# Order of the rope's work beside attention in a two-layer trunk kernel

## The chip, the cores and the metric

The kernel runs on one core of a Trainium2 chip. The metric is the device time of one execution in microseconds (us), and the figure of a kernel is the median of its runs. The core has five engines that run side by side, each in the order of its own instruction stream, and wait for one another through semaphores: TensorE (PE, matrix products), VectorE (DVE, elementwise work and reductions), ScalarE (ACT, activations and copies), GpSimd (POOL, here mostly the issue of copies) and SyncE (SP, the issue of transfers).

## The reference

The reference is a trunk of two layers over 1024 positions of width 1024, in float32. Layer 0 is attention and an MLP, layer 1 a gated recurrence and an MLP, and a norm stands at the end. The change touches layer 0's attention alone:

```
qkv = h @ w_qkv                       # q, k: 8 heads x 2 components x 64
q = rope(q, positions) * (d ** -0.5)
k = rope(k, positions)
# rope: [t1 * cos - t2 * sin, t2 * cos + t1 * sin]
s = einsum('bqhcd,bkhcd->bhcqk', qb, k)      # two score maps a head
s = where(k_chunk <= q_chunk, s, -inf)
p = softmax(s)
a = p[:, :, 0] - lam * p[:, :, 1]
o = einsum('bhqk,bkhe->bqhe', a, v)
```

So each head needs its own projected q and k, turned by the rope, before its first score.

## The kernel before

**Three products for one.** A float32 product is made of three on PE with operands cut into a high and a low part (`split`, L336): high by high, high by low, low by high. For the scores the parts are laid on top of one another. A head's component has 64 rows, so high and low part fill the 128 rows of one operand: `stacked` (L695) builds such a tile with two copies by DMA from POOL's queue. A head needs two such tiles for q (`qs`, 4 copies) and four for k (`ks`, 8 copies, 256 KB each).

**Attention in 64 slots.** `attention` (L893) walks through 8 heads of 8 query blocks, one block a slot; the blocks of a head come in the order 4, 5, 6, 7, 0, 1, 2, 3 (`ORDER`). A slot s does: scores of its block on PE (`scores`, L749: two products into each of two accumulators, then a mask and a maximum on DVE, and the exponentials on ACT), the transposes of the block before it (L809 on PE, copied out by ACT in L987), the product with v of the block two before (L819), and `combine` (L789: three DVE instructions that join the two softmaxes). Between them PE is given `fills`: steps of the projections of later heads (L588 to L591), and towards the end of the output product. PE, ACT, DVE and POOL keep the order in which the program writes the instructions (`manual_schedule`, L958); SP's order comes from a scheduler.

**The rope's work.** When a projection of q or k of a later head is done, ACT copies it out (L713), four DMAs on SP's queue copy it with its halves swapped into a tile `sw` (L668), and then five steps follow: times cos in place (DVE, L679), `sw` times sin (DVE, L680), their sum (DVE, L676), the high part (ACT, L687), the low part (DVE, L690). The low part is followed by the stack's copies on POOL (L699, L700). The product with cos writes over q or k, which the swap's DMAs read; so it waits for them.

**The queue.** The DVE steps are not written where they become ready. `aside` (L865) puts each into a list, with the slot from which it may run: it counts forward from the present slot until the given time has passed, at 2.8 + 0.65 i us for a slot of block i. The time is `RS` (10) for cos, sin and sum, `RL` (2) for the low part. `run_aside` (L876) is called twice in a slot, once after the exponentials and once after `combine`, and each call runs one step (`ASIDE`): the first in the list that is due. New entries go to the end of the list. The list also holds the scaling of attention's outputs (`subln`, L824) and their low parts (L848).

Of the kernel before, what the change touches and what calls it, by code (L numbers as in the profile page):

```python
# [12 lines left out]
ALU = mybir.AluOpType  # L13
# [281 lines left out]
class Trunk:  # L295
# [375 lines left out]
    def rope(self, q, sw, then):  # L671

        nc = self.nc

        def add():
            nc.vector.tensor_tensor(out=q, in0=q, in1=sw, op=ALU.add)  # L676
            then()

        self.aside(RS, lambda: nc.vector.tensor_tensor(out=q, in0=q, in1=self.cos, op=ALU.mult))  # L679
        self.aside(RS, lambda: nc.vector.tensor_tensor(out=sw, in0=sw, in1=self.sin, op=ALU.mult))  # L680
        self.aside(RS, add)

    def parts_of(self, q, then):

        nc = self.nc
        h, l = self.t4("qkh", F32R), self.t4("qkl", F32R)
        nc.scalar.activation(out=h, in_=q, func=AF.Copy)  # L687

        def low():
            nc.vector.tensor_tensor(out=l, in0=q, in1=h.bitcast(F32), op=ALU.subtract)  # L690
            then(h, l)

        self.aside(RL, low)

    def stacked(self, name, first, second, c):  # L695

# [165 lines left out]
            s += 1  # L862
        self.tasks.setdefault(s, []).append(fn)

    def aside(self, us, fn):  # L865

        if self.slot is None:
            self.held.append(fn)
            return
        s = self.slot  # L870
        while us > 0:
            us -= 2.8 + 0.65 * ORDER[s % NT]
            s += 1
        self.queue.append((s, fn))

    def run_aside(self, n):  # L876
        for at, fn in list(self.queue):
# [609 lines left out]
        self.mlp(1, True)  # L1487


RS, RL, RN, RT, R3 = (10, 2, 3, 2, 3)  # L1490
ASIDE = (1, 1)
LAGS = (1, 2, 4)
FILL_PART = [(1.24, 1.17, 0.33), (0.74, 1.39, 0.4), (0.52, 1.0, 0.14), (0.74, 1.26, 0.4), (0.74, 1.0, 0.56), (0.79, 0.94, 0.37), (0.89, 1.18, 0.4), (1.04, 1.23, 0.4)]
# [37 lines left out]
```

## Time and profile before

| | |
|---|---|
| median of 3 runs | 2242.0 us (2241.39 to 2243.5) |
| the profiled execution | 2248.95 us, of which span 2247.2 us |
| PE busy | 2130.8 us (95%) |
| DVE busy | 1530.5 us (68%) |
| ACT busy | 1067.6 us (48%) |
| POOL busy | 100.1 us (4%) |
| mean granted TensorE clock | 0.981 |

Attention's first score stands at 116 us, its last at 567 us. A row of the timeline gives the start from the span's beginning, the duration, engine, line, operation, the tiles written and read, and in brackets the idle time of that engine just before, with what ended it. A row of waits gives what waited, for whom, the sum, how often and the longest. In the windows, busy time of each engine is followed by the number of its instructions; PEclk is the granted TensorE clock, where 1.00 is 2.4 GHz and 0.50 is 1.2 GHz.

### The profile page before, as it was taken

Reading aid. Unit: us, or ns where it says so; the run is one execution under the profiler, and the core shown is the slowest. Engines: PE = TensorE matmul, PEld = TensorE weight load, DVE = VectorE, ACT = ScalarE, POOL = GpSimd, SP = SyncE. Lnnn points to the kernel's source line nnn. Section 1 sums busy time; section 2 is a strip of 40 time slices with the busy share of each in tenths; the row PEclk is TensorE's granted clock in tenths of the full one; section 3 lists DMA queues with packets and bytes.
Section 4 is the critical chain, followed back from the end, with each engine's and each line's share of the span. In section 5 each row is a group of like instructions: output and inputs, shape, how many; then the busy total and the mean of one; then the engine's idle time right before and its main releaser. Section 6 shows DMA issues by size and latency. Waiting matters only on the chain.

```text
span 2247.2 us, 26498 instructions
## 1 busy us (share of the span) xinstructions
PE 2130.8 (95%) x9826; PEld 1758.0 (78%) x9826; DVE 1530.5 (68%) x2073; ACT 1067.6 (48%) x1627; POOL 100.1 (4%) x171
## 2 busy tenths in 40 slices
PE   8997999879999999899999999999899999899997
PEld 7786777768888888788887887777688888688885
DVE  5465676565896777577878477756967776486575
ACT  4344566456663444344435266635644443453343
POOL 3201111110000000000000000000000000000000
PEclk9998999999999999999999999999999999999998
DMA  6635353453634443597647322144244444874633
GB/s 188 175 88 130 97 143 101 123 152 109 211 116 142 155 155 134 190 353 280 218 158 240 90 78 84 36 159 132 94 151 155 150 150 169 322 263 166 217 128 135
DMA packets 239298, 355.82 MB, mean 158 GB/s; under 512 B 16225, under 2 KB 137154, under 8 KB 239170
## 3 DMA queue, kind: packets, MB, share of 16 engines
q1 hardware_dynamic: 230338, 326.87, 43.6%
q0 software_dynamic: 7680, 25.17, 4.8%
q10 hardware_dynamic: 1152, 2.10, 0.3%
q8 instruction: 77, 1.26, 0.2%
q14 instruction: 51, 0.42, 0.1%
HBM read 229.29 MB, written 91.23 MB: 143 GB/s over the span
## 4 chain that ended last, share of the span: by engine, by line
PE 60%; DVE 11%; ACT 7%; issue 3%; DMA 2%; POOL 0%; SPq 0%; ACTq 0%; POOLq 0%; DVEq 0%
PE acc L1219 5%; PE acc L1220 5%; PE acc L1221 5%; PE acc L144 4%; PE acc L145 4%; PE acc L143 4%; PE acg L1219 2%; PE acg L1221 2%; PE acg L1220 2%; PE acc L589 2%; PE acc L588 2%; PE acb L145 2%; PE acb L143 2%; PE acb L144 2%; PE acg L145 2%
## 5 line engine op out<-in xcount | busy, mean ns | idle before, releaser
L1121 ACT ACTIVATE ct<-ct 128x1024 f32<-128x1024 f32 x64 | 67.9, 1061 | 251.1 <-DVE ct L1190 250.1
L345 DVE TENSOR_TENSOR h2l<-h,h2h 128x1024 fp32r<-128x1024 f32 x112 | 136.6, 1220 | 65.6 <-ACT h2h L342 61.9
L766 ACT ACTIVATE p<-acc,nmax 128x768 f32<-128x768 f32 (+7 forms) x128 | 95.3, 744 | 143.1 <-DVE nmax L783 71.5
L588 PE MATMUL acg<-xgh,wh 128*128 128x512 f32 x384 | 161.6, 421 | 1.5 <-ACT vT L732 1.5
L589 PE MATMUL acg<-xgl,wh 128*128 128x512 f32 x384 | 152.7, 398 | 0.0
L591 PE MATMUL acg<-xgh,wl 128*128 128x512 f32 x384 | 152.7, 398 | 0.0
L342 ACT ACTIVATE h2h<-h 128x1024 fp32r<-128x1024 f32 x112 | 117.6, 1050 | 59.6 <-DMA h<-hid 51.3
L342 ACT ACTIVATE w2h<-w 128x1024 fp32r<-128x1024 f32 x80 | 84.3, 1054 | 88.0 <-DVE w L56 72.1
L143 PE MATMUL acc<-w2h,h2h 128*128 128x512 f32 x256 | 103.0, 402 | 13.9 <-ACT w2h L342 12.2
L143 PE MATMUL acc<-h2h,w2h 128*128 128x512 f32 x256 | 101.1, 395 | 7.5 <-ACT w2h L342 7.4
L418 POOL TENSOR_TENSOR rstd<-ms,mhalf 128x4 f32<-128x4 f32 (+2 forms) x25 | 22.4, 897 | 1900.0 <-DVE ms L416 1898.6
L144 PE MATMUL acc<-w2l,h2h 128*128 128x512 f32 x256 | 102.3, 400 | 2.8 <-DVE w2l L345 2.8
L1220 PE MATMUL acc<-t12l,w12h 128*128 128x512 f32 x256 | 100.7, 393 | 4.4 <-DVE t12l L345 4.4
L1190 DVE TENSOR_TENSOR cl<-cl,acc 128x512 f32<-128x512 f32 x64 | 60.8, 950 | 64.3 <-PE acc L1221 64.3
L345 DVE TENSOR_TENSOR w2l<-w,w2h 128x1024 fp32r<-128x1024 f32 x80 | 97.7, 1222 | 9.0 <-PE acc L144 4.9
L145 PE MATMUL acc<-h2h,w2l 128*128 128x512 f32 x256 | 100.9, 394 | 2.7 <-DVE w2l L345 2.7
L1219 PE MATMUL acc<-t12h,w12h 128*128 128x512 f32 x256 | 100.6, 393 | 3.1 <-DVE ct L1190 3.1
L145 PE MATMUL acc<-w2h,h2l 128*128 128x512 f32 x256 | 101.5, 396 | 0.0
L144 PE MATMUL acc<-h2l,w2h 128*128 128x512 f32 x256 | 100.8, 394 | 0.0
L1221 PE MATMUL acc<-t12h,w12l 128*128 128x512 f32 x256 | 100.2, 391 | 0.0
L762 PE MATMUL acc<-ks,qs 128*128 128x512 f32 (+2 forms) x192 | 67.8, 360 | 23.0 <-DMA ks<-qkh 23.0
L591 PEld LDWEIGHTS acg<-xgh,wl 128*128 128x128 f32 x384 | 73.8, 192 | 17.0 <-DVE wl L345 0.5
(383 smaller groups left out, 6004.4 us busy)
## 6 DMA issues: line engine op xcount, KB each, us to landing
w<-in_mlp_w_dram SPq DMA_DIRECT2D x96, 512.0 KB, 4.4
raw<-in_mlp_w_dram SPq DMA_DIRECT2D x64, 512.0 KB, 4.4
h<-hid SPq DMA_DIRECT2D x64, 512.0 KB, 5.2
h<-hid SPq DMA_DIRECT2D x96, 256.0 KB, 5.1
w<-in_mlp_w_dram SPq DMA_DIRECT2D x80, 256.0 KB, 3.9
hid<-cl SPq DMA_DIRECT2D x64, 256.0 KB, 2.3
hid<-h SPq DMA_DIRECT2D x32, 512.0 KB, 2.6
hid<-h SPq DMA_DIRECT2D x64, 256.0 KB, 2.4
```

Source lines behind the costliest of these rows:

```text
L143: mm(bank[m], ah, bh, start=first, stop=False)
L144: mm(bank[m], ah, bl, start=False, stop=False)
L145: mm(bank[m], al, bh, start=False, stop=end)
L342: nc.scalar.activation(out=hi, in_=src, func=AF.Copy)
L345: (lo_eng or nc.vector).tensor_tensor(out=lo, in0=src, in1=hi.bitcast(F32), op=ALU.subtract)
L588: mm(ps[:, pc], a, xh[:, cs], start=(k == 0), stop=False)
L589: mm(ps[:, pc], a, xl[:, cs], start=False, stop=False)
L591: mm(ps[:, pc], b, xh[:, cs], start=False, stop=(k == n - 1))
L766: nc.scalar.activation(out=p[c][:, :n], in_=src, func=AF.Exp, bias=nmax[:, c : c + 1], accum_out=sums[:, c : c + 1])
L1219: mm(bank, ah[:, k], bh, start=k == 0, stop=False)
L1220: mm(bank, ah[:, k], bl, start=False, stop=False)
L1221: mm(bank, al[:, k], bh, start=False, stop=k == 3)
```

## The change

Three edits in the queue: the product with cos gets the waiting time `RL` (2) instead of `RS`; `RS` falls from 10 to 5, for sin and sum; and the low part is put at the head of the list instead of its end. No instruction is added or removed.

```diff
-        self.aside(RS, lambda: nc.vector.tensor_tensor(out=q, in0=q, in1=self.cos, op=ALU.mult))
+        self.aside(RL, lambda: nc.vector.tensor_tensor(out=q, in0=q, in1=self.cos, op=ALU.mult))
         self.aside(RS, lambda: nc.vector.tensor_tensor(out=sw, in0=sw, in1=self.sin, op=ALU.mult))
         self.aside(RS, add)
...
-        self.aside(RL, low)
+        self.aside(RL, low, True)
...
-    def aside(self, us, fn):
+    def aside(self, us, fn, soon=False):
...
-        self.queue.append((s, fn))
+        self.queue.insert(0 if soon else len(self.queue), (s, fn))
...
-RS, RL, RN, RT, R3 = (10, 2, 3, 2, 3)
+RS, RL, RN, RT, R3 = (5, 2, 3, 2, 3)
```

DVE around the low part of head 1's k (`qkl<-k_1060`), before: it stands in slot 7, between the maximum and the `combine` of a block of 512 columns.

```order
L773 MEMSET acc_1555 64x2x64
L774 TENSOR_REDUCE nmax<-acc_1555 128x2
L690 TENSOR_TENSOR qkl_1441<-k_1060,qkh_1440 128x1024
L794 RECIPROCAL rsum<-sums 128x2
L796 SCALAR_TENSOR_TENSOR fac<-sums,rsum,neglam 128x1
L797 SCALAR_TENSOR_TENSOR p_1553<-p_1554,fac,p_1553 128x512
```

The same instruction in the changed kernel: it stands in slot 5, with a block of 256 columns.

```order
L773 MEMSET acc_1455 64x2x64
L774 TENSOR_REDUCE nmax<-acc_1455 128x2
L690 TENSOR_TENSOR qkl_1417<-k_1060,qkh_1416 128x1024
L794 RECIPROCAL rsum<-sums 128x2
L796 SCALAR_TENSOR_TENSOR fac<-sums,rsum,neglam 128x1
L797 SCALAR_TENSOR_TENSOR p_1453<-p_1454,fac,p_1453 128x256
```

It moved two slots ahead. The low parts of k of heads 2 to 7 stand in slots 11, 21, 28, 38, 45, 52 before and 10, 20, 27, 37, 44, 51 now; those of q of heads 1 to 7 in 5, 8, 20, 25, 35, 44, 51 before and 3, 7, 17, 24, 34, 41, 48 now.

POOL's queue at the copies of head 1, before: head 1's q stack, then the power that gives `rstd` for the outputs of head 0, then the k stack.

```order
L699 DMA qs_1471<-qkh_1338 64x1024
L700 DMA qs_1471<-qkl_1339 64x1024
L418 TENSOR_TENSOR rstd<-ms,mhalf 128x4
L699 DMA ks_1585<-qkh_1440 64x1024
L700 DMA ks_1585<-qkl_1441 64x1024
L699 DMA ks_1588<-qkh_1440 64x1024
```

The same place in the changed kernel, to the first copy of head 2's q.

```order
L700 DMA qs_1346<-qkl_1278 64x1024
L699 DMA ks_1476<-qkh_1416 64x1024
L700 DMA ks_1476<-qkl_1417 64x1024
L699 DMA ks_1479<-qkh_1416 64x1024
L700 DMA ks_1479<-qkl_1417 64x1024
L699 DMA ks_1482<-qkl_1417 64x1024
L700 DMA ks_1482<-qkh_1416 64x1024
L699 DMA ks_1485<-qkl_1417 64x1024
L700 DMA ks_1485<-qkh_1416 64x1024
L418 TENSOR_TENSOR rstd<-ms,mhalf 128x4
L699 DMA qs_1598<-qkh_1537 64x1024
```

The whole k stack passed `rstd`.

DVE in slot 21, at the product with cos of head 4's q (`q_2243` before, `q_2249` now). Before, the slot holds a scaling of outputs and, after `combine`, a low part:

```order
L828 TENSOR_TENSOR o_231_1618<-o_231_1618,rstd 128x512
L794 RECIPROCAL rsum<-sums 128x2
L796 SCALAR_TENSOR_TENSOR fac<-sums,rsum,neglam 128x1
L797 SCALAR_TENSOR_TENSOR p_2499<-p_2500,fac,p_2499 128x256
L690 TENSOR_TENSOR qkl_2454<-k_2054,qkh_2453 128x1024
```

Now:

```order
L774 TENSOR_REDUCE nmax<-acc_2524 128x2
L679 TENSOR_TENSOR q_2249<-q_2249,cos_723 128x1024
L794 RECIPROCAL rsum<-sums 128x2
L796 SCALAR_TENSOR_TENSOR fac<-sums,rsum,neglam 128x1
L797 SCALAR_TENSOR_TENSOR p_2522<-p_2523,fac,p_2522 128x256
```

The product with cos moved from slot 23 to slot 21, one slot after its projection, and stands ahead of that slot's `combine`.

## Rows read from the trace of the kernel before

**Rows 1.** The page: engines' busy time, share of the span, instructions.

```profile
PE 2130.8 (95%) x9826; PEld 1758.0 (78%) x9826; DVE 1530.5 (68%) x2073; ACT 1067.6 (48%) x1627; POOL 100.1 (4%) x171
```

**Rows 2.** Waits of PE from 110 to 585 us.

```profile
PE acc L762 <- DMA ks<-qkh: 23.0, 7, 8.5
PE acb L809 <- DVE p L797: 13.9, 8, 3.0
```

**Rows 3.** Timeline of PE at the first scores of heads 1, 3, 5, 6.

```profile
178.56 0.77 PE L762 MATMUL acc<-ks,qs 128*128 128x512 f32 x1 [8.47 <-DMA ks<-qkh]
...
288.01 0.47 PE L762 MATMUL acc<-ks,qs 128*128 128x512 f32 x1 [1.24 <-DMA ks<-qkh]
...
397.83 0.77 PE L762 MATMUL acc<-ks,qs 128*128 128x512 f32 x1 [5.63 <-DMA ks<-qkh]
400.64 0.77 PE L762 MATMUL acc<-ks,qs 128*128 128x512 f32 x1 [1.30 <-DMA ks<-qkh]
...
462.01 0.47 PE L762 MATMUL acc<-ks,qs 128*128 128x512 f32 x1 [3.86 <-DMA ks<-qkh]
```

**Rows 4.** Windows around these waits: start and end, length, busy times, PEclk.

```profile
173.40:186.80 13.40, 7.47 (x21) 5.98 (x22) 4.14 (x6) 2.29 (x4) 1.64 (x4) 0.50 0.58 139
187.00:200.00 13.00, 13.00 (x76) 11.16 (x74) 9.55 (x17) 8.24 (x21) 0.51 (x1) 1.00 0.36 97
395.20:405.30 10.10, 6.17 (x16) 4.98 (x17) 2.05 (x5) 0.88 (x2) 0.00 (x0) 0.50 0.53 129
...
463.50:470.10 6.60, 5.46 (x17) 4.61 (x18) 2.50 (x4) 1.28 (x3) 0.00 (x0) 0.50 0.30 89
```

**Rows 5.** Timeline of DVE: the maxima in slots 5 and 20, low parts of k.

```profile
157.43 0.69 DVE L774 TENSOR_REDUCE nmax<-acc 128x2 f32<-128x512 f32 x1
...
168.38 1.22 DVE L690 TENSOR_TENSOR qkl<-k,qkh 128x1024 fp32r<-128x1024 f32 x1
...
266.57 0.42 DVE L774 TENSOR_REDUCE nmax<-acc 128x2 f32<-128x256 f32 x1
...
274.30 1.22 DVE L690 TENSOR_TENSOR qkl<-k,qkh 128x1024 fp32r<-128x1024 f32 x1
```

**Rows 6.** The same in slots 37 and 44.

```profile
378.04 0.69 DVE L774 TENSOR_REDUCE nmax<-acc 128x2 f32<-128x512 f32 x1
...
387.48 1.22 DVE L690 TENSOR_TENSOR qkl<-k,qkh 128x1024 fp32r<-128x1024 f32 x1
...
434.54 0.42 DVE L774 TENSOR_REDUCE nmax<-acc 128x2 f32<-128x256 f32 x1
...
443.82 1.23 DVE L690 TENSOR_TENSOR qkl<-k,qkh 128x1024 fp32r<-128x1024 f32 x1 [1.02 <-DMA qs<-qkh]
```

**Rows 7.** Timeline of POOL: head 1's k stack, second and last copy.

```profile
170.11 0.51 POOL L700 DMA_DIRECT2D ks<-qkl  x1 [3.60 <-DVE qkl L690]
...
173.18 0.52 POOL L700 DMA_DIRECT2D ks<-qkh  x1
```

**Rows 8.** Landing of L700's copies, 165 to 183 us, then 443 to 466 us.

```profile
DMA to landing us min/median/max: 2.9/5.7/7.5
...
DMA to landing us min/median/max: 6.9/12.3/15.6
```

**Rows 9.** Line 679 in the whole trace: how DVE waited for the swap.

```profile
  DMA sw<-q: 2.4, 1
  DMA sw<-k: 1.0, 1
```

**Rows 10.** The swap of head 4's q (270 to 277 us), and DVE's slot 21.

```profile
L668 SPq DMA_DIRECT2D sw<-q x4: 513/587/1118, 270.3 to 272.2; - x4
...
DMA to landing us min/median/max: 2.2/2.3/3.9
...
271.45 0.69 DVE L774 TENSOR_REDUCE nmax<-acc 128x2 f32<-128x512 f32 x1
```

**Rows 11.** Waits of POOL from 110 to 585 us.

```profile
POOL qs L699 <- ACT o L820: 51.0, 1, 51.0
```

## The prediction

> **What bounds the kernel now.** The page comes first: PE is busy for 95% of the span and DVE for 68% [rows 1], so what PE waits for is what an edit of DVE's order can give back, and the next view is the waits of PE over attention alone, 110 to 585 us [rows 2]. Its first line is the largest: 23.0 us in 7 waits, where the first score of a head stands until the copies of `ks` have landed. The second is 13.9 us for `combine`. The timeline then says where: heads 1, 3, 5 and 6 start late, with 8.47, 1.24, 5.63 and 3.86 us in front of the first matmul [rows 3], and three of them wait a second time a few matmuls later for the last copy, head 5 1.30 us [rows 3], so heads 1 and 6 together 2.5 us, what is left of 23.0. Heads 2, 4 and 7 start without a wait.
>
> The waits cost more than their own length. In the windows from 173.4, 395.2 and 463.5 us the granted clock is 0.50, that is 1.2 GHz, and it is back at 1.00, 2.4 GHz, in the windows after [rows 4]. In those three windows PE worked 7.47, 6.17 and 5.46 us, together 19.1 us. At the full clock the same work takes half, so 9.55 us are given back if the clock doesn't fall there. Waits and clock together: 23.0 + 9.55 = 32.6 us. That is the most that this change can take from the `ks` waits.
>
> Here the Trainium skill has a rule of its own: in "TensorE: Matmul & The Clock Gate", section Terms, the penalty is about the throttled time multiplied by the missing share of the clock. For 13.4 + 10.1 + 6.6 = 30.1 us at half clock it gives 15.05 us, and the sum would be 38.1 us. The rows decide: PE stood idle in 11.0 of those 30.1 us, and this idle time is in the 23.0 us already.
>
> **The change part by part.** It adds and removes nothing, so every cost is one of order.
>
> *Low parts of k earlier.* Head 1's low part of k starts at 168.38 us. In the changed order it stands behind the maximum of slot 5, which ended at 157.43 + 0.69 = 158.1 us, so 10.3 us sooner [rows 5]. For heads 3, 5 and 6 the same reading (slots 20, 37 and 44) gives 274.30 - 266.99 = 7.3 us, 387.48 - 378.73 = 8.75 us and 443.82 - 434.96 = 8.9 us [rows 5, 6]. The copies follow the low part at POOL's pace: head 1's second copy is issued at 170.11, when the low part is done, the last at 173.18 us [rows 7], and the last landing takes 7.5 us, so 180.7 us [rows 8], where PE's second wait ends. With 10.3 us less it is 170.4 us; PE comes to this head at 178.56 - 8.47 = 170.1 us and needs the last copy after four more matmuls. So head 1's waits go, barely. Head 6 waits 3.86 us and a second time at most 2.5, against 8.9 us won; head 5 5.63 and 1.30 against 8.75; head 3 1.24 against 7.3. All four are covered, if the copies keep their distance from the low part. Head 6 has the loosest reading: its last copies took up to 15.6 us to land, where head 1's took 7.5 [rows 8]. In the old order its q stack was issued only a few us ahead of its k stack (k's low part even waited 1.02 us for a q copy [rows 6]); in the new one q's low part stands three slots before k's (41 and 44; before 44 and 45), so I expect its landing to be sooner, not later.
>
> *q's low parts earlier.* No wait of PE names `qs` [rows 2], so this gives nothing by itself; it clears POOL's queue.
>
> *The product with cos earlier, at one slot from its projection.* This adds a wait: cos overwrites what the swap reads. Where cos was late, DVE waited for a swap twice only, 2.4 and 1.0 us, both in the first head's work ahead of attention [rows 9]. Laid over the old times, the new places of cos come after the swap's landing for 11 of the 14 q and k. The clear exception is head 4's q in slot 21: its swap is issued from 270.3 to 272.2 us and lands 2.2 to 3.9 us later, so at 274.4 to 276.1, while DVE comes to cos when the maximum ends, at 271.45 + 0.69 = 272.1 us [rows 10]. DVE would stand 2.3 to 4.0 us there, with `combine` of that slot queued behind it, and PE's transposes of the next slot wait for that. Two others, the k of heads 6 and 7, are close. Bounds of the sum: nothing, if the waits fall into idle time of DVE, to 7 us, if all three are as long as the 2.3 us and reach PE. Between them I take 3 us, near head 4's wait alone, the one that the rows show.
>
> *Sin and sum earlier.* Each of the 14 keeps its 1.2 us of DVE and one step per call of the queue, so a `combine` has at most one step in front of it, as before. Their new neighbours change which `combine` is late. The row that prices it is the 13.9 us in 8 waits [rows 2], 1.7 us each: two waits fewer or four more are -3.5 to +7 us. I take +1 us, since the number of steps is the same.
>
> *POOL.* The k stack passes `rstd` of the head before. `rstd` then waits until the low part is there and eight copies of 0.5 us are issued, about 5 us; its reader, the scaling on DVE, is due a slot later and is queued behind a low part in the same list. I take nothing, and up to 3 us where a scaling comes early.
>
> Sum: 32.6 - 3 - 1 = 28.6 us less. The profiled execution took 2248.95 us, 1.75 us around its span; it would become 2220.4. The median of the runs is 7 us below that execution, and the stages after attention follow it unchanged, so the same difference goes to the median: 2242.0 - 28.6 = 2213.4 us.
>
> **The rivals.**
> *Half of it.* The copies' landing, not the low part, sets the end: they land up to 15.6 us after issue [rows 8], behind the core's other transfers, and an earlier stack may meet the loads of weights and the stores of outputs. For: eight copies of head 6 were slow after all were issued. Against: head 1's were not. If heads 5 and 6 keep their waits and clock (5.63 + 1.30 + 3.86 + up to 2.5 us, and half of 6.17 + 5.46, 5.8 us), 19.1 us of the 28.6 are lost, and 9.5 us of gain are left: 2232.5 us.
>
> *The buffers decide.* A stack's tile must be free before its first copy; POOL once stood 51.0 us for an output copy that still used one [rows 11]. With other tiles in play, the k stacks may wait for readers that finish as late as the old low parts did, and nothing moves: 2242 us. Against: in the old order those long waits were of q stacks, and their end lay ahead of the low part anyway.
>
> *Slower: DVE stands for the swaps.* In DVE's stream everything behind cos waits with it, above all `combine` and the next slot's maximum, on which ACT's exponentials depend. If the swaps land later than in the old trace, because SP's stream now has other stores ahead of them, the wait of slot 21 becomes the rule. At 4.0 us for each of 14 products it is 56 us against 32.6, so 23 us slower if all reach PE: 2265 us. It decides from 32.6 / 14 = 2.3 us a product on. Against: 11 of 14 places leave room in the old times.
>
> *No such effect as said* is not among them: the orders shown do move the low parts.
>
> **How the numbers follow.** My forecast, all four heads start on time, has 0.72, with its own range of 2207 to 2221: 35 us, if nothing new is lost and some `combine` waits go too, to 21 us, with 7 us lost for swaps and 5 for `combine`. Half of it has 0.15, buffers 0.08, slower 0.05. The range that should hold 8 in 10 is 2205 to 2232. A difference under 0.2%, 4.5 us, can't be told from none. Faster: 0.72 + 0.14 and a part of the rest, 0.87; within: 0.08; slower: 0.05.
>
> **What would show it.** In the new profile, the line of `ks` waits of PE should be gone or under 3 us, and the granted clock should not fall to 0.50 at the starts of heads 1, 5 and 6. Line 679 should name the swap's DMAs as what DVE waited for, with 3 to 8 us in all. The waits of PE for `combine` should stay between 10 and 21 us. If `ks` waits remain above 10 us while the low parts stand where I read them, landing or buffers are the cause and the forecast is wrong; if line 679's waits are above 25 us, the slower rival holds.

## The result and the profile after

The changed kernel takes 2224.2 us (2222.2 to 2225.5, 4 runs), against 2242.75 us (2241.4 to 2243.7, 4 runs) for the kernel before on the same chip: a ratio of 0.9917 with an interval of 0.99 to 0.9934, 18.5 us less. The forecast was 2213.4 us, 28.6 less. The profiled execution took 2225.5 us, so it stands near its median, where that of before stood 7 us above its own.

The page after, its span and the busy times. They answer to [rows 1]: no engine has more or less to do, PE apart, whose busy time depends on its clock.

```profile
span 2223.8 us, 26505 instructions
PE 2121.7 (95%) x9826; PEld 1750.8 (79%) x9826; DVE 1530.4 (69%) x2073; ACT 1066.8 (48%) x1627; POOL 101.6 (5%) x171
```

The waits of PE from 110 to 585 us after: what waited, for whom, the sum, how often, the longest. They answer to [rows 2].

```profile
PE acb L809 <- DVE p L797: 15.9, 9, 4.6
PE acb L819 <- ACT aT L987: 9.7, 9, 2.3
PE acb L838 <- ACT aT L987: 6.1, 6, 1.7
PE acb L741 <- ACT aT L987: 5.7, 5, 1.7
PE acc L762 <- ACT p L766: 0.7, 1, 0.7
...
PE acc L762 <- DMA ks<-qkh: 0.3, 1, 0.3
```

The same view of before had these lines below the two shown:

```profile
PE acb L741 <- ACT aT L987: 5.7, 5, 1.7
PE acb L819 <- ACT aT L987: 5.5, 8, 1.8
PE acb L838 <- ACT aT L987: 4.2, 4, 2.0
```

The line that was the largest, 23.0 us for `ks`, is down to 0.3 us. But the line for `combine` (L809) and two of the three for ACT's copies of the transposes (`aT`) have grown. Attention's stretch, from its first score to its last, gives the balance. First before, then after; busy time of each engine, then granted clock:

```profile
116.25:566.90 450.65, 399.20 (x2203) 337.50 (x2201) 289.89 (x508) 248.05 (x631) 58.52 (x99) 0.95 0.45 118
```

```profile
115.07:546.40 431.33, 393.78 (x2203) 332.57 (x2202) 290.06 (x508) 247.49 (x631) 60.07 (x99) 0.98 0.45 123
```

The stretch is 19.3 us shorter. (The last score stands 20.5 us sooner, but 1.2 us of that lie ahead of the first score, which moves between 115.1 and 116.5 us from kernel to kernel.) PE's idle time in it (length less PE's busy time) fell from 51.45 to 37.55 us, 13.9 us; its busy time fell by 5.4 us for the same 2203 matmuls. The idle time is the `ks` waits, 22.7 us less, and all the rest, 28.4 us before and 37.2 us after, 8.8 us more. So the gain at the heads' starts is all there, and 40% of it was given back in other waits.

The fall of the busy time is mostly the clock. Outside the stretches of [rows 4], before had three more at half clock in attention; after has three in all, and the three of [rows 4] have no counterpart. Before, the three others:

```profile
371.30:374.50 3.20, 2.97 (x9) 2.58 (x10) 2.16 (x5) 2.80 (x7) 0.00 (x0) 0.50 0.00 0
453.20:456.50 3.30, 2.67 (x8) 2.31 (x9) 2.48 (x4) 1.28 (x4) 0.00 (x0) 0.50 1.03 277
538.60:541.80 3.20, 3.20 (x12) 2.57 (x11) 2.64 (x6) 2.85 (x6) 0.44 (x1) 0.50 0.08 29
```

After, all three:

```profile
269.80:276.40 6.60, 5.57 (x15) 4.55 (x16) 4.67 (x12) 3.52 (x9) 0.75 (x1) 0.50 0.03 9
365.30:372.00 6.70, 6.03 (x23) 5.45 (x23) 2.58 (x5) 3.29 (x9) 0.00 (x0) 0.50 0.10 39
413.10:416.30 3.20, 3.20 (x12) 2.73 (x11) 3.12 (x5) 1.02 (x2) 0.00 (x0) 0.50 0.27 110
```

If half of PE's busy time at half clock is lost, as the prediction reckons, that is (19.1 + 8.8) / 2 = 14.0 us before and 14.8 / 2 = 7.4 us after, a difference of 6.6 us, where 5.4 were measured. Half is a little too much. In the stretch at 269.8 us a matmul of 512 columns starts every 0.43 us (L589 at 273.00, L591 at 273.42 us), and at the full clock every 0.23 us (L588 at 277.61, L589 at 277.84 us), so 0.46 of the busy time is lost, and the difference becomes 6.1 us. The 0.7 us that are left stay unexplained.

The new stretch at 269.8 us leads to the largest single loss. DVE around it, after (start, duration, what; in brackets the idle time before, and what ended it):

```profile
260.45 0.69 DVE L774 TENSOR_REDUCE nmax<-acc 128x2 f32<-128x512 f32 x1
268.61 1.23 DVE L679 TENSOR_TENSOR q<-q,cos 128x1024 f32<-128x1024 f32 x1 [7.47 <-DMA sw<-q]
...
270.20 0.48 DVE L797 SCALAR_TENSOR_TENSOR p<-p,fac,p 128x256 f32<-128x256 f32 x1
```

PE at the same place, then ACT:

```profile
270.83 0.66 PE L809 MATMUL acb<-ident,p 128*128 128x128 f32 x2 [4.59 <-DVE p L797]
```

```profile
271.94 0.58 ACT L766 ACTIVATE p<-acc,nmax 128x384 f32<-128x384 f32 x1 [6.52 <-DVE nmax L774]
```

It is the place that the forecast named, slot 21 and the product with cos of head 4's q. DVE stands 7.47 us for the swap, `combine` is queued behind it, PE stands 4.59 us for `combine`, and then works 5.57 us at 1.2 GHz. The swap itself had become slow. Its four copies, after: durations of the issues on SP's queue and landings.

```profile
L668 SPq DMA_DIRECT2D sw<-q x4: 512/2073/2560, 258.1 to 263.4; - x4
DMA to landing us min/median/max: 7.4/8.3/9.2
```

Before they were issued in 1.9 us and landed in 2.2 to 3.9 us [rows 10]. What else was in flight is seen on POOL: the stack of head 3's k, which before was issued after this swap, now stands just ahead of it. (The first of its eight copies had landed, in 3.1 us, before the swap was issued at 258.1 us; the other seven were issued from 255.7 to 259.0 us.)

```profile
252.52 0.57 POOL L699 DMA_DIRECT2D ks<-qkh  x1 [9.50 <-ACT o L820]
255.73 0.51 POOL L700 DMA_DIRECT2D ks<-qkl  x1 [2.64 <-DVE qkl L690]
...
258.96 0.51 POOL L700 DMA_DIRECT2D ks<-qkh  x1
```

### The profile page after: what moved, and what is told of

Same layout as the page of the kernel before. It is cut to its first block, busy times and chain, and to the rows that moved or that the text cites. A ratio compares the mean times of both kernels' runs of the same rounds, so it can differ in the third digit from the quotient of the medians.

```text
span 2223.8 us, 26505 instructions
## 1 busy us (share of the span) xinstructions
PE 2121.7 (95%) x9826; PEld 1750.8 (79%) x9826; DVE 1530.4 (69%) x2073; ACT 1066.8 (48%) x1627; POOL 101.6 (5%) x171
## 4 chain that ended last, share of the span: by engine, by line
PE 68%; DVE 14%; ACT 9%; issue 4%; DMA 3%; SPq 1%; POOL 0%; ACTq 0%; DVEq 0%; POOLq 0%
PE acc L1219 5%; PE acc L1220 5%; PE acc L1221 5%; PE acc L145 4%; PE acc L144 4%; PE acc L143 4%; PE acg L588 3%; PE acg L591 3%; PE acg L589 3%; PE acg L1219 2%; PE acg L1221 2%; PE acg L1220 2%; PE acc L589 2%; PE acc L591 2%; PE acc L588 2%
## 5 line engine op out<-in xcount | busy, mean ns | idle before, releaser
L588 PE MATMUL acg<-xgh,wh 128*128 128x512 f32 x384 | 160.5, 418 | 1.5 <-ACT vT L732 1.5
L591 PE MATMUL acg<-xgh,wl 128*128 128x512 f32 x384 | 152.0, 396 | 0.0
L589 PE MATMUL acg<-xgl,wh 128*128 128x512 f32 x384 | 151.9, 396 | 0.0
L591 PEld LDWEIGHTS acg<-xgh,wl 128*128 128x128 f32 x384 | 73.2, 191 | 16.4 <-DVE wl L345 0.2
L588 PEld LDWEIGHTS acg<-xgh,wh 128*128 128x128 f32 x384 | 73.6, 192 | 12.9 <-ACT vT L732 1.9
```

Source lines behind the costliest of these rows:

```text
L588: mm(ps[:, pc], a, xh[:, cs], start=(k == 0), stop=False)
L589: mm(ps[:, pc], a, xl[:, cs], start=False, stop=False)
L591: mm(ps[:, pc], b, xh[:, cs], start=False, stop=(k == n - 1))
```

## The experiments

The theory: the `ks` waits and their clock went as forecast; what is missing is lost in waits that the early product with cos adds, above all in slot 21, where the earlier k stack and the swap share the transfer engines. The rival: the product with cos is harmless, and the new waits come of the other steps' order. Letters in the expectations stand for the theory (A) and what is set against it, each time as it bears on that edit. Ratios are against the kernel before on the same chip. For an edit that is made on the changed kernel, the difference of its ratio to 0.9917 is given in us (0.001 is 2.24 us); the two intervals together leave about 5 us of doubt on such a difference.

**No wait for the swap.** The product goes into a tile of its own, so that it needn't wait for the swap's reads.

```diff
+        t = []
+
+        def cos():
+            t.append(self.t4("qc"))
+            nc.vector.tensor_tensor(out=t[0], in0=q, in1=self.cos, op=ALU.mult)
         def add():
-            nc.vector.tensor_tensor(out=q, in0=q, in1=sw, op=ALU.add)
-            then()
+            nc.vector.tensor_tensor(out=t[0], in0=t[0], in1=sw, op=ALU.add)
+            then(t[0])
-        self.aside(RL, lambda: nc.vector.tensor_tensor(out=q, in0=q, in1=self.cos, op=ALU.mult))
+        self.aside(RL, cos)
...
-        self.rope(t, sw, lambda: self.parts_of(t, stack))
+        self.rope(t, sw, lambda r: self.parts_of(r, stack))
```

> The changed kernel, but the product with cos goes to a tile of its own, so it no longer waits until the swap's DMAs have read q or k; every step keeps its slot. Theory A (DVE's waits for the swap at the product with cos, 16 us in the changed kernel's attention, are what the forecast missed): these waits go, those left move to the product with sin and stay under 3 us, PE's wait of 4.6 us for combine at 271 us goes with the half clock behind it, and the time falls by 7 to 12 us, to 2212 to 2217. Rival B (once the ks waits are gone, PE meets other waits for combine and for ACT's copies whatever cos does): the waits for the swap go too, but the time stays at 2224 within 3 us.

Measured: 2220.3 us, ratio 0.9885 (0.9872 to 0.9899), 7 us better than the change. No product waits for a swap in attention any more. But the new tile waits twice for copies that still read its buffer, 4.43 and 1.31 us, and the longer of these waits stands at the very place in question, head 4's q in slot 21:

```profile
266.56 1.23 DVE L678 TENSOR_TENSOR qc<-q,cos 128x1024 f32<-128x1024 f32 x1 [4.43 <-DMA ks<-qkl]
```

So DVE's wait there was made shorter, from 7.47 to 4.43 us, and not taken away. It was enough: PE's wait for that `combine` fell from 4.59 to 1.55 us, and the clock does not fall there. PE's first two lines (numbers of lines are 5 higher here):

```profile
PE acb L814 <- DVE p L802: 13.0, 9, 3.0
PE acb L824 <- ACT aT L992: 9.7, 11, 2.3
```

The theory holds for the first line, which is back near the 13.9 us of before. The second is as large as in the changed kernel with no swap waited for: most of those 4 us more are not the swap's, and here the rival has a part.

**Only one product later.** The changed kernel, with head 4's q alone kept at the old waiting time.

```diff
-    def rope(self, q, sw, then):
+    def rope(self, q, sw, then, wait=None):
...
-        self.aside(RL, lambda: nc.vector.tensor_tensor(out=q, in0=q, in1=self.cos, op=ALU.mult))
+        self.aside(RL if wait is None else wait, lambda: nc.vector.tensor_tensor(out=q, in0=q, in1=self.cos, op=ALU.mult))
...
-        self.rope(t, sw, lambda: self.parts_of(t, stack))
+        self.rope(t, sw, lambda: self.parts_of(t, stack), 10 if (h, kind) == (4, "q") else None)
```

> The changed kernel, but head 4's q alone gets its product with cos two slots later (slot 23 instead of 21); its low part keeps slot 24 and every other step keeps its slot. Theory A: that one wait of 7.5 us is the one that reaches PE whole; slot 22 shrinks from 12 to some 6 us, no half clock at 270 us, and the time falls by 6 to 8 us, to 2216 to 2218. Rival B: 2224 within 2 us, since another wait takes its place.

Measured: 2219.5 us, ratio 0.9886 (0.9871 to 0.9901), the same as with all swap waits away. What DVE still waits for, and PE's waits for `combine` and for `aT`:

```profile
DVE k L679 <- DMA sw<-k: 9.1, 5, 3.3
```

```profile
PE acb L809 <- DVE p L797: 11.4, 8, 3.0
PE acb L819 <- ACT aT L987: 9.3, 9, 2.3
```

So the one wait of 7.47 us costs all that was won back. The 9.1 us of swap waits in five other places cost no more that can be measured than the 5.7 us of buffer waits that stood in their stead in the experiment before.

How much of a wait is free in slot 21 can be read here, where no product stands in it. `combine` waits for ACT's exponentials anyway:

```profile
265.87 0.17 DVE L794 RECIPROCAL rsum<-sums 128x2 f32<-128x2 f32 x1 [3.62 <-ACT p L766]
```

Of these 3.62 us the product itself takes 1.23; the other 2.4 us can be waited away. What goes beyond them reaches PE: of 7.47 us that is 5.1 (PE stood 4.59), of the 4.43 us with a tile of its own it is 2.0 (PE stood 1.55). The 2.3 to 4.0 us that the prediction read for this place would, by this estimate, have cost PE 0 to 1.6 us.

In the traces attention, from its first score to its last, takes 5.1 us less than in the changed kernel (426.2 against 431.3 us); the medians say 7, with their 5 us of doubt.

**The stack out of the swap's way.** The changed kernel, with the low part of head 3's k put to the end of slot 21, behind the product with cos, so that its copies come later.

```diff
-    def parts_of(self, q, then):
+    def parts_of(self, q, then, late=None):
...
-        self.aside(RL, low, True)
+        if late is None:
+            self.aside(RL, low, True)
+        else:
+            self.queue.append((late, low))
...
-        self.rope(t, sw, lambda: self.parts_of(t, stack))
+        self.rope(t, sw, lambda: self.parts_of(t, stack, 21.5 if (h, kind) == (3, "k") else None))
...
-    def run_aside(self, n):
+    def run_aside(self, n, half=0):
-            if n and (at <= self.slot or self.slot >= H * NT):
+            if n and (at <= self.slot + half or self.slot >= H * NT):
...
-                self.run_aside(ASIDE[1] if h < H else 4)
+                self.run_aside(ASIDE[1] if h < H else 4, 0.5)
```

> The changed kernel, but the low part of head 3's k alone is put off to the end of slot 21 (its old place), behind the product with cos of head 4's q, which stays in the middle of slot 21; all other steps keep their slots. It tells why that product waited 7.5 us. Theory A1 (the swap of head 4's q took 9.8 us from its first issue to its last landing because the copies of head 3's k stack, moved one slot ahead, were under way on the same 16 DMA engines): the swap now takes 3 to 5 us, DVE waits under 3 us there, slot 22 loses its 4.6 us wait and the half clock; head 3's ks wait of 1 to 2 us comes back; time 5 us less, 2217 to 2221. Rival B1 (the swap is slow for another reason, such as its place in SP's stream): DVE's wait stays at 6 us or more and the time at 2224 within 2 us.

Measured: 2222.6 us, ratio 0.9895 (0.988 to 0.9911), about 5 us better than the change, as much as the doubt; in the traces attention, from its first score to its last, takes 2.4 us less (428.9 against 431.3 us). What the swap did is plainer than the time. The swap of head 4's q in this kernel, its issues and landings, and the product that waits for it:

```profile
L668 SPq DMA_DIRECT2D sw<-q x4: 513/586/593, 258.1 to 259.9; - x4
DMA to landing us min/median/max: 2.2/2.3/2.3
```

```profile
263.39 1.23 DVE L679 TENSOR_TENSOR q<-q,cos 128x1024 f32<-128x1024 f32 x1 [2.28 <-DMA sw<-q]
```

The swap is issued at the same time as in the changed kernel, from 258.1 us. With seven of the stack's copies out of its way it lands in 2.3 us, not 8.3, and DVE stands 2.28 us. So it is the stack in flight that made the swap slow. The `ks` wait of head 3, expected back, did not come: PE's list has no line for `ks` here.

**All products at once.** To see whether the mechanism of the prediction's rival "Slower" is real: the changed kernel with the product with cos due without any delay.

```diff
-        self.aside(RL, lambda: nc.vector.tensor_tensor(out=q, in0=q, in1=self.cos, op=ALU.mult))
+        self.aside(0, lambda: nc.vector.tensor_tensor(out=q, in0=q, in1=self.cos, op=ALU.mult))
```

> The changed kernel, but the product with cos is due at once, in the slot of its projection, 0 to 2 slots earlier than in the changed kernel. Theory A: DVE stands for the swap nearly every time, 3 to 5 us for most of 14, 35 us or more in all; a good part reaches PE, and the time is 2235 to 2260. Rival B: no more than 4 us from 2224.

Measured: 2257.5 us, ratio 1.0049 (1.0037 to 1.0062): slower than the kernel before, though no wait for `ks` is left. DVE's waits at the product, then PE's first two lines:

```profile
DVE q L679 <- DMA sw<-q: 31.9, 6, 11.1
DVE k L679 <- DMA sw<-k: 9.2, 3, 6.0
```

```profile
PE acb L819 <- ACT aT L987: 24.7, 12, 6.7
PE acb L809 <- DVE p L797: 20.7, 9, 6.4
```

DVE stands 41 us for swaps, and PE's waits for `aT` and `combine` grow together by 20 us over the changed kernel's. The mechanism is real; how early the product stands decides whether it bites.

**The low part alone.** The kernel before, with the low part at the head of the list and nothing else.

```diff
-        self.aside(RL, low)
+        self.aside(RL, low, True)
...
-    def aside(self, us, fn):
+    def aside(self, us, fn, soon=False):
...
-        self.queue.append((s, fn))
+        self.queue.insert(0 if soon else len(self.queue), (s, fn))
```

> The first kernel with one edit alone: the low part goes to the head of the list; RS stays 10 for cos, sin and sum. The low parts of k of heads 1, 3, 5, 6 stand in the middle of slots 6, 21, 38, 45 (before: 7, 21 end, 38 end, 45 end; changed: 5, 20, 37, 44), which in the old times is 5.3, 2.3, 3.2 and 3.7 us sooner. Theory A: about 13 of the 23 us of ks waits go, heads 1 and 5 keep some 4 us each and head 6 2 us, no wait for the swap at cos; 14 to 18 us less than the kernel before, about as much as the whole change. Rival B (earlier low parts do not pay by themselves): under 8 us less.

Measured: 2227.2 us, ratio 0.9917 (0.9905 to 0.9929), the ratio of the whole change. PE's waits for `ks` that are left, at the first scores of heads 1 and 5 (head 6, expected to keep 2 us, keeps none):

```profile
174.06 0.58 PE L762 MATMUL acc<-ks,qs 128*128 128x512 f32 x1 [3.69 <-DMA ks<-qkh]
391.16 0.76 PE L762 MATMUL acc<-ks,qs 128*128 128x512 f32 x1 [4.60 <-DMA ks<-qkh]
```

The other two edits take these 8.3 us away and bring new waits: together they are worth nothing that the medians can tell, with the doubt of 5 us. In the traces attention, from its first score to its last, takes 4.4 us longer here than in the changed kernel (435.7 against 431.3 us), so a small gain of theirs is not excluded.

**The shorter time for sin and sum alone.** The kernel before with `RS` at 5, for cos, sin and sum.

```diff
-RS, RL, RN, RT, R3 = (10, 2, 3, 2, 3)
+RS, RL, RN, RT, R3 = (5, 2, 3, 2, 3)
```

> The first kernel with RS = 5 alone (cos, sin and sum all at 5, low part at the end of the list). The low parts of k of heads 1, 3, 5, 6 stand in slots 6, 20 end, 38 end, 44. Theory A: the ks waits of heads 3 and 6 go, head 5 keeps its 6.9 us, head 1 some 4; no wait for the swap beyond 4 us; 10 to 17 us less than the kernel before. Rival B: under 6 us less.

Measured: 2245.3 us, ratio 0.9997 (0.9988 to 1.0007): no change, where the theory wanted a gain. The waits for `ks` did fall by 11.5 us, to 11.5 us, but PE's other waits grew by about as much. The largest of these is one that no one had on the list, on ACT and then on PE:

```profile
474.14 0.63 ACT L845 ACTIVATE ohl<-ot 128x512 fp32r<-128x512 f32 x1 [7.57 <-DMA qs<-qkh]
```

```profile
478.50 1.51 PE L809 MATMUL acb<-ident,p 128*128 128x128 f32 x6 [7.54 <-DVE p L797]
```

**The product back at the time of sin and sum.** The changed kernel with cos at `RS`, which is 5.

```diff
-        self.aside(RL, lambda: nc.vector.tensor_tensor(out=q, in0=q, in1=self.cos, op=ALU.mult))
+        self.aside(RS, lambda: nc.vector.tensor_tensor(out=q, in0=q, in1=self.cos, op=ALU.mult))
```

> The changed kernel with one edit undone: the product with cos waits as long as that with sin (RS, 5). Its k low parts keep their slots but for head 5 (38 instead of 37) and head 2 (11 instead of 10). Theory A: DVE's waits for the swap fall under 5 us; head 5's ks wait comes back in part (up to 4 of its 6.9 us, with the clock); time 2215 to 2221, under the changed kernel's 2224. Rival B: 2224 to 2230, as the ks wait of head 5 comes back and nothing else is won.

Measured: 2229.1 us, ratio 0.9923 (0.9911 to 0.9935), within the doubt the same as the change. The theory's number was missed, and the rival's was met. The swap waits in attention are gone and 6.3 us of `ks` waits are back, as said, but the wait on ACT of the experiment above is here too. ACT, DVE and PE, in the order in which it travels, and the window behind it:

```profile
465.89 0.63 ACT L845 ACTIVATE ohl<-ot 128x512 fp32r<-128x512 f32 x1 [8.14 <-DMA qs<-qkh]
```

```profile
467.50 1.23 DVE L345 TENSOR_TENSOR wol<-raw,woh 128x1024 fp32r<-128x1024 f32 x1 [11.11 <-ACT woh L342]
```

```profile
470.26 1.51 PE L809 MATMUL acb<-ident,p 128*128 128x128 f32 x6 [8.11 <-DVE p L797]
```

```profile
465.60:475.40 9.80, 4.78 (x15) 3.70 (x16) 7.29 (x11) 5.06 (x11) 0.31 (x1) 0.50 0.21 81
```

ACT's instruction names a copy of head 7's q stack as what it waited for, though it reads none of it. All these tiles come from one pool (`t4`), so the tile that it writes is most likely one that this copy still read. ACT's split of a weight (`woh`) is queued behind it, DVE waits for that, `combine` waits behind DVE, and PE stands 8.11 us and then works at half clock. That another buffer would take the wait away was not tried; the cause is read from the trace alone.

**The kernel before once more**, unchanged, for a second profile.

> The kernel before, unchanged, for a second profile on another chip: its profiled execution lay 7 us above the median of its runs, and the forecast was summed on that one. If the ks waits of PE are 23 us here too, the sum was sound and the 7 us are elsewhere; if they are 18 us or less, the profiled execution was long in just what the forecast counted.

Measured: 2243.9 us, span 2242.1 us. `ks` and `combine`:

```profile
PE acc L762 <- DMA ks<-qkh: 25.3, 7, 8.6
PE acb L809 <- DVE p L797: 14.0, 8, 3.0
```

The waits of [rows 2] are there again, so the largest term stood on sound rows. Attention's last score is at 566.6 us, against 566.9 in the first profile; the 5 us by which the first profile's span was longer lie behind attention, where nothing was changed.

## Why the prediction was right in kind, and off in size

*The `ks` waits, 23.0 us.* Right: 22.7 us of them are gone. Head 1, forecast to be covered "barely", waits 0.27 us in the changed kernel's list, and 3.69 us where its low part stands later (the low part alone).

*The clock, 9.55 us.* Right at its place: no half clock at a head's start. PE's busy time fell by 5.4 us net, because half is a little too much, and because the new stretch at 269.8 us costs 5.57 / 2 = 2.8 us by the same reckoning; the others came out about even. The Trainium skill ("TensorE: Matmul & The Clock Gate", section Terms) takes the throttled time by the missing share of the clock; for 39.8 us before and 16.5 after that would be 11.7 us, against 5.4 measured in PE's busy time. The rows decide again, since PE stood idle in part of that time.

*The product with cos, taken at 3 us, from 0 to 7.* This is the term that failed. In attention DVE stood 16.3 us for swaps, in 6 waits, where the prediction said "3 to 8 us in all". The places were named (head 4's q, and the k of heads 6 and 7, with 3.02 and 3.36 us), the size of the first was not: the step laid the new places of cos "over the old times" and used the old landing, 2.2 to 3.9 us. But another part of the same change had moved head 3's k stack ahead of that very swap. Its landing became 7.4 to 9.2 us and the wait 7.47 us, which cost 4.59 us of PE and 2.8 us of clock, 7.4 us in that slot. Making the wait shorter, moving that product, or moving the stack won back 7, 7 and 5 us, each with its 5 us of doubt. It was not this slot alone: over all of attention the median landing of the swaps' copies went from 2.4 to 4.5 us. As to the other five waits, no run shows a cost of theirs, so nothing speaks against the low bound, that they fall where DVE has time to spare.

*New neighbours, taken at 1 us, from -3.5 to 7.* Too small, within the bounds. The waits for `combine` came out at 15.9 us, inside the 10 to 21 forecast, but 4.59 us of them are the swap's, and the prediction looked at that line alone. Two lines of PE for `aT` grew by 4.2 us (L819) and 1.9 us (L838). The first keeps its size when no swap is waited for; with cos at the time of sin and sum, or with the low part alone, it is 5.7 and 5.9 us. So it goes with the early product with cos and what moves with it, more than with the wait for the swap. The growth is spread over several places, not the same ones in each kernel (the largest new wait is 1.45 us, at 300 us). By which step of DVE it comes about was not taken apart.

*The sum.* With what the two traces show: -22.7 - 5.4 + 8.8 = -19.3 us, by which attention became shorter. The forecast had -23.0 - 9.55 + 4 = -28.6. In the medians it is 18.5 us; the traces' spans differ by 23.4 us, of which 1.2 lie ahead of attention and 2.9 behind it. So the time lies in the wide range, 2205 to 2232, but not in the forecast's own, 2207 to 2221, although all four heads start on time, as it said: its 7 us for swaps and 5 us for `combine` left out the waits for `aT` and the new half clock.

*The rivals.* "Half of it" did not happen: heads 5 and 6 start on time. "The buffers decide" did not happen in the changed kernel, but in two neighbours of it a reused tile, as the traces have it, cost PE 7.5 and 8.1 us, and hid what their order had won. "DVE stands for the swaps" was the right mechanism at a smaller size: in the changed kernel it took back a quarter of the gain, and with the product still earlier it made the kernel slower than before. Its reason was another, though. It feared other stores ahead of the swap on SP; a store does stand there (`ohT`, at 257.4 us), but it stands there too in the kernel with the stack later, where the swap lands in 2.3 us.

*A better version.* The changed kernel with head 4's product kept late, or with a tile of its own for the product, takes 2219 to 2220 us, ratios 0.9886 and 0.9885, and beats both the kernel before and the changed one.

## What to carry to other kernels

When one change moves both a transfer and a step that waits for another transfer, don't read the landing from the old trace: list what will be in flight at the new time, and price the wait with a landing read under such traffic. A wait of the engine that feeds the bound one is priced by what is queued behind it and by the clock that the idle time takes; here one wait of 7.5 us, 2.4 us of it free, cost as much as could be won back, and 9 us in five others cost nothing that can be measured. Try the parts of a change by themselves: one edit of three brought as much as all of them, within 5 us.

## What the runs showed of the hardware

A queue is slowed by copies that another engine issued. With seven copies of 256 KB in flight from POOL's queue, the four swap copies of 128 KB from SP's took 8.3 us (median) to land, and SP's own issue instructions up to 2.56 us. With one such copy beside them, issued at 259.5 us, it was 2.3 us, and 0.59 at most. The window of transfers from 252 to 272 us, in the changed kernel and in the one with that stack later (KB each, median us to landing):

```profile
ks<-qkh POOLq DMA_DIRECT2D x4, 256.0 KB, 6.1
sw<-q SPq DMA_DIRECT2D x4, 128.0 KB, 8.3
```

```profile
ks<-qkh POOLq DMA_DIRECT2D x4, 256.0 KB, 5.0
sw<-q SPq DMA_DIRECT2D x4, 128.0 KB, 2.3
```

The Trainium skill says in "DMA: Bandwidth & Descriptors", section Issuing engines are not separate DMA queues, that transfers from SP, ACT and POOL run on the same 16 engines and interleave. These landings agree, and the rule would have warned of this very step.
